# The opening of a decoder layer: one tile's modulation moved to TensorE, c spread by TensorE, small loads on ScalarE's queue, order of the splits fixed

## The chip, the cores and the metric

The kernel runs on one core of one Trainium2 chip. A core has TensorE (PE, matrix products; PEld is its loading of the stationary operand), VectorE (DVE), ScalarE (ACT), GpSimd (POOL) and SyncE (SP, which here only issues DMA transfers). The metric is the device time of one execution in microseconds, lower is better; the median of several runs is given. All numbers are in microseconds unless it is said otherwise.

## The reference, cut to what matters

The reference is one decoder layer on x (512 x 1024, float32) with a conditioning vector c (1024). What the change touches is at its very beginning:

```python
mod = c @ w_ada + b_ada                      # 1024 -> 6 * 1024
sh1, sc1, gt1, sh2, sc2, gt2 = split(mod, 6)
u = x * (1.0 + sc1) + sh1
proj = u @ w_in                              # q, k, v, forget logits, gates of two attention branches
log_f = log_sigmoid(f_a + b_forget)
# two causal attention branches (softmax with forget decay; stick-breaking),
# each projected to 1024, merged by sigmoid gates, times w_o
x = layer_norm(ALPHA * x + (1 + gt1) * attn_out)
u2 = x * (1.0 + sc2) + sh2
h = causal_depthwise_conv(u2 @ w_up)         # width 3
x = layer_norm(ALPHA * x + (1 + gt2) * ((silu(h_gate) * h_val) @ w_down))
```

So the first products with w_in need u, u needs sc1 and sh1, and these need c and two sixths of w_ada.

## The kernel before, in words

Products in float32 precision are made of three faster ones: each operand is split into a high part (a rounding copy, `hi_of`, on ScalarE) and a low part (the difference, `lo_of`, on VectorE), and high times high, high times low and low times high are added up in PSUM. Both helpers record one line for all their uses, so in the profile the splits are told apart by their tiles: `wh` and `wl` are the parts of a weight tile `raw`, `uh` and `ul` those of a tile of u.

The opening works on the eight channel tiles of 128 channels, j = 0 to 7. u is held with channels on partitions, so that scale and shift are one number per partition. For each j the kernel

- loads two 128 x 1024 tiles `wa` of w_ada (its transpose: one row per channel), the rows of x for these channels (`xt`, 128 x 512) and the first 904 columns of w_in (`raw`): `first_load`, all on SP's queue;
- sums each `wa` against c, which lies spread over all partitions in `cbc`, into one number per partition, and adds the bias: `first_acc` and `mod_col`, on VectorE. The result is `modc`;
- splits `raw`: `first_split`, and for the pieces that come late `first_pad`, which also fills the eight forget columns in `fpad`;
- makes `uh` on ScalarE from `xt` with scale and bias, then u in place of `xt` on VectorE, then `ul` as their difference: `first_mod`. The in-place u has to wait until ScalarE has read `xt`;
- issues 23 products, spread over eight PSUM banks (`grp`) that add up over j: `first_mm`.

For j = 0 the sums are made in two halves of 512 columns, as the pieces come in. The first half of `cbc` is loaded by a DMA that repeats the row of c over all partitions. The second half is spread by TensorE, a product of a row of ones and the row `cbr`, and copied out of PSUM by ScalarE.

The order on SP's queue is that of the program text. The order of the other engines is planned by a scheduler that works with its own costs; `tc.issue_after(x)` ties what is issued within it behind x. DMA transfers share a ring of eight semaphores, so that the ninth waits for the first. Tiles come from pools with a fixed number of buffers: five for `wa`, four for `raw` (`LOADS`), three for each of `wh` and `wl` (`WBUFS`).

Behind the opening come the attention heads, with further projections as filler between them, the merge and w_o, the first norm, the up projection with the convolution, and the down projection with the last norm. Their code isn't touched, but for `mod_col`, which later tiles of w_ada use as well and which loses a parameter that they don't set.

Of the kernel before, what the change touches and what calls it, by code (L numbers as in the profile page):

```python
# [8 lines left out]
F32 = mybir.dt.float32  # L9
F32R = mybir.dt.float32r  # L10
BF16 = mybir.dt.bfloat16
# [5 lines left out]
P = 128  # L17
# [21 lines left out]
LATE = 6  # L39
EARLY = 2  # L40
CUT = 5
FILL = (13, 13, 13), (11, 11, 11)


@with_exitstack
def layer_kernel(ctx: ExitStack, tc: tile.TileContext, out, xT, x, cT, crow, wa0, wa1, bcol, bgt, w1, wct, wv, bf,
                 wp, wo, lncol, lnrow, wup, cwb, wdn):
# [32 lines left out]
    cbc = const([P, D], F32, "cbc")  # L80
    cbr = early.tile([1, 512], F32, name="cbr", tag="cbr")
    nc.sync.dma_start(cbr, crow[:, 512:1024])
# [7 lines left out]
    S.activation(sgt, ones[:, 0:1], AF.Sigmoid)  # L90
    make_identity(nc, ident)
# [64 lines left out]
    G.memset(fl(fpad), 0.0)  # L156
    PE.matmul(grp[0], ones[0:1, :], cbr, start=True, stop=True)
    S.activation(cbc[:, 512:1024], grp[0], AF.Copy)

    def mod_col(w, col, wt, parts=1):  # L160
        raw = modr[:, w, col, :]
        n = D // parts
        for e in range(parts):
            c = slice(e * n, (e + 1) * n)
            V.scalar_tensor_tensor(wt[:, c], wt[:, c], 1.0, cbc[:, c], ALU.mult, ALU.mult, accum_out=raw[:, e : e + 1])
        b, o = bcols[:, w, col : col + 1], modc[:, w, col : col + 1]
        if parts == 1:
            V.tensor_tensor(o, raw[:, 0:1], b, ALU.add)
        else:
            V.scalar_tensor_tensor(o, raw[:, 0:1], raw[:, 1:2], b, ALU.add, ALU.add)  # L170

    def first_load(j):
        wa = [early.tile([P, D], F32, name=nm("wa"), tag="wa", bufs=5) for _ in range(2)]
        r = stg.tile([P, 1024], F32, name=nm("raw"), tag="raw", bufs=LOADS)
        xt = z(F32, "xt")
        if j == 0:
            for e in range(2):
                c = slice(e * 512, (e + 1) * 512)
                if e == 0:
                    nc.sync.dma_start(cbc[:, c], crow[:, c].broadcast_to([P, 512]))  # L180
# [4 lines left out]
            for c in (slice(0, 384), slice(384, W1C)):  # L185
                nc.sync.dma_start(r[:, c], w1[j][:, c])
            nc.sync.dma_start(cTs, cT)
            nc.sync.dma_start(bfs, bf)
        else:
            nc.sync.dma_start(r[:, 0:W1C], w1[j])  # L190
            nc.sync.dma_start(xt, xT[j * P : (j + 1) * P, :])
            for q in range(2):
                nc.sync.dma_start(wa[q], wa0[j, q])
        pend[j] = [wa, xt, r]

    def first_acc(j):
        wa = pend[j][0]
        if j == 0:
            for q in (1, 3):
                V.tensor_scalar_add(bcols[:, q, :], bcols[:, q, :], 1.0)  # L200
        mod_col(0, j, wa[0], 2 if j == 0 else 1)
        mod_col(1, j, wa[1], 2 if j == 0 else 1)

    def first_split(j):
        r = pend[j][2]
# [3 lines left out]
        if j:  # L209
            lo_of(l[:, 0:W1C], r[:, 0:W1C], h[:, 0:W1C])  # L210
        pend[j][2:] = [h, l, r]
# [11 lines left out]
    def first_mod(j):  # L223
        wa, xt = pend[j][0:2]
        sh, sc = modc[:, 0, j : j + 1], modc[:, 1, j : j + 1]
        a, b = z(F32R, "uh"), z(F32R, "ul")
        u = S.activation(a, xt, AF.Identity, bias=sh, scale=sc)
        V.tensor_scalar(xt, xt, sc, sh, ALU.mult, ALU.add)
        state["after"] = lo_of(b, xt, a)
        if j == 0:  # L230
            with tc.issue_after(u.ins):
                first_pad(j)
        else:
            first_pad(j)
        uh.append(a)
        ul.append(b)
# [746 lines left out]
def _pack(inputs):  # L983
# [18 lines left out]
    def col(kind, n):  # L1002
        if kind in ("sb", "fox"):
# [23 lines left out]

_NAMES = ["xT", "x", "cT", "crow", "wa0", "wa1", "bcol", "bgt", "w1", "wct", "wv", "bf", "wp", "wo", "lncol", "lnrow",
          "wup", "cwb", "wdn"]
# [19 lines left out]
```

## Time and profile before

| | |
|---|---|
| median of 3 runs | 772.62 us (772.52 to 773.3) |
| the profiled execution: time, and span of its core | 772.12 us, 770.3 us |
| TensorE busy | 748.1 us, 97% of the span |
| VectorE busy | 549.4 us, 71% |
| ScalarE busy | 350.4 us, 45% |
| GpSimd busy | 185.7 us, 24% |
| loaded from HBM | 96.88 MB |
| first product of channel tile 0 starts at | 10.46 us |
| first product of channel tile 7 starts at | 49.26 us |

The page of the profile gives each engine's busy time, then the span in 40 slices with the busy share in tenths. The timeline rows give the start, the length, the engine, the line of the code and the operation as out<-in, with the number of instructions that the row merges; in brackets stands the idle time of the engine before it and what ended that. The ends of products are modelled and overlap the next one's start, so the pace of products is read from their starts.

### The profile page before, as it was taken

The page shows a single profiled execution, that of the slowest core. Times are in us where ns is not written, and L with a number is a line of the kernel's source. Part 1 is how long each engine was busy: PE and PEld are TensorE (multiplying, and loading weights), DVE is VectorE, ACT ScalarE, POOL GpSimd, SP SyncE. Part 2 cuts the span into 40 slices and gives each one's busy share as a digit, 9 for nine tenths or more (in the row PEclk, how much of TensorE's full clock was granted, in tenths as well). Part 3 has the DMA queues.
Part 4 walks back from the last instruction along what each step waited for, and adds up shares of the span by engine and source line. Part 5 has one row for each costly group of instructions (what it writes and reads, how often), then busy time and mean ns, then how long its engine had stood idle before and what let it go on. Part 6 is the DMA issues. An engine that isn't in the chain of part 4 may idle for free.

```text
span 770.3 us, 9560 instructions
## 1 busy us (share of the span) xinstructions
PE 748.1 (97%) x3556; PEld 620.6 (81%) x3556; DVE 549.4 (71%) x822; ACT 350.4 (45%) x583; POOL 185.7 (24%) x138
## 2 busy tenths in 40 slices
PE   5998999999999999999999999999999999999995
PEld 3886887788888888888889888888888888888885
DVE  6979889966687977776676787686656665533666
ACT  3357686717667556333145434444444433222400
POOL 1025424510000011364000780000000043945500
PEclk9999999999999999999999999999999999999998
DMA  8951253542333323455302524354332214323202
GB/s 310 403 204 55 83 165 131 175 161 83 110 110 110 127 93 136 144 190 164 137 1 73 201 79 145 118 177 137 114 105 93 100 55 165 120 98 127 65 28 83
DMA packets 31105, 99.68 MB, mean 129 GB/s; under 512 B 4273, under 2 KB 4785, under 8 KB 31058
## 3 DMA queue, kind: packets, MB, share of 16 engines
q1 hardware_dynamic: 30546, 99.00, 37.0%
q8 instruction: 28, 0.46, 0.2%
q14 instruction: 19, 0.16, 0.1%
q0 software_dynamic: 512, 0.07, 0.1%
HBM read 96.88 MB, written 2.10 MB: 128 GB/s over the span
## 4 chain that ended last, share of the span: by engine, by line
PE 86%; DVE 6%; ACT 5%; DMA 1%; issue 1%; SPq 0%; DVEq 0%; ACTq 0%
PE ps L110 17%; PE ps L111 17%; PE ps L112 17%; PE ps L941 5%; PE ps L940 5%; PE ps L942 5%; PE ps L254 4%; PE ps L495 2%; PE ps L821 2%; PE ps L820 2%; PE ps L819 2%; PE ps L477 2%; DVE om L456 1%; DMA wa<-in_wa 1%; ACT wh L75 1%
## 5 line engine op out<-in xcount | busy, mean ns | idle before, releaser
L78 DVE TENSOR_TENSOR wl<-raw,wh 128x1024 fp32r<-128x1024 f32 (+2 forms) x106 | 143.8, 1357 | 101.0 <-ACT wh L75 100.5
L75 ACT ACTIVATE wh<-raw 128x1024 fp32r<-128x1024 f32 (+2 forms) x106 | 110.4, 1042 | 108.1 <-PE ps L942 39.9
L110 PE MATMUL ps<-u2h,wh 128*128 128x512 f32 (+1 forms) x376 | 141.4, 376 | 0.0
L111 PE MATMUL ps<-u2l,wh 128*128 128x512 f32 (+1 forms) x376 | 141.2, 376 | 0.0
L112 PE MATMUL ps<-u2h,wl 128*128 128x512 f32 (+1 forms) x376 | 141.2, 375 | 0.0
L587 POOL TENSOR_TENSOR raw<-raw,gt 128x1024 f32<-128x1024 f32 x22 | 60.7, 2774 | 187.1 <-DVE gt L550 157.6
L110 PE MATMUL ps<-uh,wh 128*128 128x512 f32 x232 | 92.9, 400 | 2.2 <-DVE vv L78 2.2
L112 PE MATMUL ps<-uh,wl 128*128 128x512 f32 x232 | 90.8, 391 | 0.0
L111 PE MATMUL ps<-ul,wh 128*128 128x512 f32 x232 | 90.8, 391 | 0.0
L110 PEld LDWEIGHTS ps<-u2h,wh 128*128 128x128 f32 x376 | 70.8, 188 | 12.9
L111 PEld LDWEIGHTS ps<-u2l,wh 128*128 128x128 f32 x376 | 70.8, 188 | 12.8
L112 PEld LDWEIGHTS ps<-u2h,wl 128*128 128x128 f32 x376 | 70.8, 188 | 12.6
L110 PEld LDWEIGHTS ps<-uh,wh 128*128 128x128 f32 x232 | 43.6, 188 | 10.7 <-DVE vv L78 2.5
L112 PEld LDWEIGHTS ps<-uh,wl 128*128 128x128 f32 x232 | 43.6, 188 | 9.4
L111 PEld LDWEIGHTS ps<-ul,wh 128*128 128x128 f32 x232 | 43.7, 188 | 7.9
L940 PE MATMUL ps<-wh,hh 128*128 128x512 f32 x128 | 49.8, 389 | 0.0
L941 PE MATMUL ps<-wl,hh 128*128 128x512 f32 x128 | 49.8, 389 | 0.0
L942 PE MATMUL ps<-wh,hl 128*128 128x512 f32 x128 | 49.8, 389 | 0.0
L457 POOL TENSOR_TENSOR pt<-pt,om 128x127 f32<-128x127 f32 (+3 forms) x32 | 40.0, 1278 | 33.8 <-DVE om L456 28.7
L75 ACT ACTIVATE hh<-cv 128x512 fp32r<-128x512 f32 x22 | 13.9, 631 | 59.6 <-DVE cv L920 59.6
L575 POOL TENSOR_TENSOR raw<-raw,gt 128x1024 f32<-128x1024 f32 x8 | 21.1, 2645 | 78.0 <-DVE m L78 42.2
L919 ACT ACTIVATE cv<-cv 128x512 f32<-128x512 f32 x22 | 13.9, 632 | 54.5 <-DVE cv L914 54.5
(188 smaller groups left out, 1463.0 us busy)
## 6 DMA issues: line engine op xcount, KB each, us to landing
raw<-in_wup SPq DMA_DIRECT2D x44, 512.0 KB, 3.3
raw<-in_wa SPq DMA_DIRECT2D x32, 512.0 KB, 3.3
raw<-in_wct SPq DMA_DIRECT2D x29, 512.0 KB, 3.2
raw<-in_wdn SPq DMA_DIRECT2D x22, 512.0 KB, 3.2
wa<-in_wa SPq DMA_DIRECT2D x14, 512.0 KB, 8.7
raw<-in_wp SPq DMA_DIRECT2D x8, 512.0 KB, 3.3
raw<-in_wo SPq DMA_DIRECT2D x8, 512.0 KB, 3.6
raw<-in_w SPq DMA_DIRECT2D x7, 452.0 KB, 8.3
```

What stands on the lines that cost most here:

```text
L75: S.activation(o, i, AF.Copy, scale=scale)
L78: return V.tensor_tensor(o, i, fl(hi), ALU.subtract)
L110: PE.matmul(ps, wh, ah, start=first, stop=False)
L111: PE.matmul(ps, wh, al, start=False, stop=False)
L112: PE.matmul(ps, wl, ah, start=False, stop=last)
L254: PE.matmul(grp[g], w, u, start=j == 0 and n == 0, stop=j == KT - 1 and n == (1 if g == 7 else 2))
L457: G.tensor_tensor(pt[b][:, s : e - 1], pt[b][:, s : e - 1], om[:, s + 1 : e], ALU.mult)
L575: G.tensor_tensor(r, r, gt[0], ALU.mult)
L587: G.tensor_tensor(r, r, gt[1], ALU.mult)
L940: PE.matmul(ps, hh[j][:, tb], w[0], start=first, stop=False)
L941: PE.matmul(ps, hh[j][:, tb], w[1], start=False, stop=False)
L942: PE.matmul(ps, hl[j][:, tb], w[0], start=False, stop=last)
```

## The change

Four things change, all in the opening:

1. The modulation of tile 0 is summed by TensorE. Its two tiles now come from w_ada itself (`wam`, contraction on partitions), and for each of shift and scale eight products of a 128 x 128 block with one column of c (`cTs`) add up in one column of a bank; VectorE adds the bias to both. They are in plain float32. `wa0` keeps the tiles 1 to 7.
2. c is spread by TensorE alone: a tile `crz` of zeros, with c in its first row, is multiplied by a 128 x 128 matrix of ones, in two products of 512 columns, and ScalarE copies both to `cbc`. VectorE zeroes `crz` (it takes one of the `wa` buffers), and the DMA of c waits for that. Before them stand three products on another zeroed tile (`WARM = 3`, bf16, 512 columns), whose result isn't used.
3. The small inputs (`cTs`, `bcols`, `bfs` and the row of c) are loaded on ScalarE's queue, ahead of its table load; SP's queue begins with the tiles of `wam`. For tile 1 the loads are put in another order.
4. The order on the engines is tied: the split of tile j + 1 behind `uh` of tile j on ScalarE, the sums of tile j + 1 behind `ul` of tile j on VectorE; for tile 1 its low parts behind its `modc`.

```diff
+    S.dma_start(cTs, cT)
...
+    S.dma_start(bcols, bcol)
+    crz = early.tile([P, D], F32, name="crz", tag="wa", bufs=5)
+    V.memset(crz, 0.0)
+    crd = S.dma_start(crz[0:1, :], crow)
+    warm = early.tile([P, 512], BF16, name="warm", tag="warm")
+    V.memset(warm, 0.0)
...
-    PE.matmul(grp[0], ones[0:1, :], cbr, start=True, stop=True)
-    S.activation(cbc[:, 512:1024], grp[0], AF.Copy)
...
+    for n in range(WARM):
+        PE.matmul(grp[4], warm[:, 0:P], warm, start=True, stop=True)
+    for e in range(2):
+        PE.matmul(grp[e], ones, crz[:, e * 512 : (e + 1) * 512], start=True, stop=True)
+        S.activation(cbc[:, e * 512 : (e + 1) * 512], grp[e], AF.Copy)
...
         if j == 0:
-            for e in range(2):
-                c = slice(e * 512, (e + 1) * 512)
-                if e == 0:
-                    nc.sync.dma_start(cbc[:, c], crow[:, c].broadcast_to([P, 512]))
-                for q in range(2):
-                    nc.sync.dma_start(wa[q][:, c], wa0[j, q][:, c])
-            nc.sync.dma_start(bcols, bcol)
+            for q in range(2):
+                for e in range(2):
+                    c = slice(e * 512, (e + 1) * 512)
+                    nc.sync.dma_start(wa[q][:, c], wam[q][:, c])
+            nc.sync.dma_start(r[:, 0:384], w1[j][:, 0:384])
             nc.sync.dma_start(xt, xT[j * P : (j + 1) * P, :])
...
+            nc.sync.dma_start(r[:, 384:W1C], w1[j][:, 384:W1C])
+            S.dma_start(bfs, bf)
+        elif j == 1:
+            nc.sync.dma_start(wa[0], wa0[j - 1, 0])
+            nc.sync.dma_start(r[:, 0:W1C], w1[j])
+            nc.sync.dma_start(wa[1], wa0[j - 1, 1])
+            nc.sync.dma_start(xt, xT[j * P : (j + 1) * P, :])
...
-        mod_col(0, j, wa[0], 2 if j == 0 else 1)
-        mod_col(1, j, wa[1], 2 if j == 0 else 1)
+            mps = grp[2]
+            for q in range(2):
+                for k in range(KT):
+                    PE.matmul(mps[:, q : q + 1], wa[q][:, k * P : (k + 1) * P], cTs[:, k : k + 1], start=k == 0, stop=k == KT - 1)
+            V.tensor_tensor(modc[:, 0:2, 0], mps[:, 0:2], bcols[:, 0:2, 0], ALU.add)
+            return
+        mod_col(0, j, wa[0])
+        state["modc"] = mod_col(1, j, wa[1])
...
+        if j == 1:
+            h, l, r = pend[j][2:]
+            with tc.issue_after(state["modc"].ins):
+                state["after"] = lo_of(l[:, 0:W1C], r[:, 0:W1C], h[:, 0:W1C])
         a, b = z(F32R, "uh"), z(F32R, "ul")
-        u = S.activation(a, xt, AF.Identity, bias=sh, scale=sc)
-        V.tensor_scalar(xt, xt, sc, sh, ALU.mult, ALU.add)
+        u = state["u"] = S.activation(a, xt, AF.Identity, bias=sh, scale=sc)
+        with tc.issue_after(state["after"].ins) if j == 1 else ExitStack():
+            V.tensor_scalar(xt, xt, sc, sh, ALU.mult, ALU.add)
         state["after"] = lo_of(b, xt, a)
-        if j == 0:
-            with tc.issue_after(u.ins):
-                first_pad(j)
-        else:
+        with tc.issue_after(u.ins):
             first_pad(j)
...
         if j + 1 < KT:
-            first_split(j + 1)
-            first_acc(j + 1)
+            with tc.issue_after(state["u"].ins) if j else ExitStack():
+                first_split(j + 1)
+            with tc.issue_after(state["after"].ins):
+                first_acc(j + 1)
...
-    r["wa0"] = c(wt[0:2].transpose(1, 0, 2, 3))
+    r["wa0"] = c(wt[0:2, 1:].transpose(1, 0, 2, 3))
+    r["wam"] = c(wk[:, :, 0:2, 0:P].transpose(2, 1, 0, 3).reshape(2, P, D))
```

More of the change, by code (lines that the diff above doesn't have):

```diff
@@ L40 @@
 EARLY = 2
+WARM = 3
 CUT = 5
@@ L45, in layer_kernel @@
 @with_exitstack
-def layer_kernel(ctx: ExitStack, tc: tile.TileContext, out, xT, x, cT, crow, wa0, wa1, bcol, bgt, w1, wct, wv, bf,
+def layer_kernel(ctx: ExitStack, tc: tile.TileContext, out, xT, x, cT, crow, wam, wa0, wa1, bcol, bgt, w1, wct, wv, bf,
                  wp, wo, lncol, lnrow, wup, cwb, wdn):
@@ L89, in layer_kernel @@
     sgt = const([P, 1], F32, "sgt")
-    S.activation(sgt, ones[:, 0:1], AF.Sigmoid)
+    with tc.issue_after(crd.ins):
+        S.activation(sgt, ones[:, 0:1], AF.Sigmoid)
     make_identity(nc, ident)
@@ L156, in layer_kernel, with mod_col @@
     G.memset(fl(fpad), 0.0)
-    PE.matmul(grp[0], ones[0:1, :], cbr, start=True, stop=True)
-    S.activation(cbc[:, 512:1024], grp[0], AF.Copy)
[L160 to L168, printed above, removed]
-        else:
-            V.scalar_tensor_tensor(o, raw[:, 0:1], raw[:, 1:2], b, ALU.add, ALU.add)
+    for n in range(WARM):
[3 more added lines that the diff above has]
+        S.activation(cbc[:, e * 512 : (e + 1) * 512], grp[e], AF.Copy)
+    def mod_col(w, col, wt):
+        raw = modr[:, w, col, 0:1]
+        V.scalar_tensor_tensor(wt, wt, 1.0, cbc, ALU.mult, ALU.mult, accum_out=raw)
+        return V.tensor_tensor(modc[:, w, col : col + 1], raw, bcols[:, w, col : col + 1], ALU.add)
     def first_load(j):
```

13 lines of the change are left out of this document (3 added, 10 removed).

## The prediction

> **What bounds the kernel now.** I read the page's engine shares first, then busy time by stretches of the opening, then the opening's timeline engine by engine, then the rows of the nearest priced instructions.
>
> ```profile
> span 770.3 us, 9560 instructions
> ...
> PE 748.1 (97%) x3556; PEld 620.6 (81%) x3556; DVE 549.4 (71%) x822; ACT 350.4 (45%) x583; POOL 185.7 (24%) x138
> ...
> PE   5998999999999999999999999999999999999995
> ```
>
> TensorE is the bound over the whole kernel; only the first slice (19 us) has a visible hole. A change of the opening is worth what it moves the moment from which TensorE runs without a hole. By stretches (columns: window, length, then busy us and instruction count of PE, PEld, DVE, ACT, POOL, granted clock, DMA share, GB/s):
>
> ```profile
> 10.50:17.40 6.90, 6.90 (x24) 5.31 (x24) 5.66 (x13) 2.47 (x6) 0.00 (x0) 1.00 1.01 374
> ...
> 28.20:33.40 5.20, 5.20 (x25) 4.30 (x24) 5.20 (x12) 1.88 (x3) 0.00 (x0) 1.00 1.03 402
> ```
>
> From 28 us on one channel tile (23 products) takes 5.20 us of a full TensorE. VectorE is full as well, and the DMA engines are. The first tile took 6.9. TensorE's own timeline, start and length in front:
>
> ```profile
> 2.24 2.04 PE L157 MATMUL ps<-cbr,ones 1*128 1x512 f32 x2 [2.24 <-DMA cbr<-in_crow]
> 10.46 1.65 PE L254 MATMUL ps<-uh,wh 128*128 128x512 f32 x3 [6.18 <-ACT uh L227]
> ...
> 13.89 0.62 PE L254 MATMUL ps<-wl,uh 128*128 128x512 f32 x2
> ```
> ```profile
> 49.26 0.39 PE L254 MATMUL ps<-uh,wh 128*128 128x512 f32 x1
> ```
>
> Tile 0 starts at 10.46. Its first eight products take 3.43 us, 0.43 each; after 13.89 the pace is 0.23 (5.20/23). The granted clock column says 1.00 for that window, so the slow start is read from the pace alone. The last tile (7) starts at 49.26, and everything behind it keeps its order in the changed kernel. So I forecast one number: when tile 7 starts after the change. What holds a tile's start is its `uh`, hence VectorE and ScalarE. From tile 1 to tile 2 they ran thus:
>
> ```profile
> 16.32 0.16 DVE L168 TENSOR_TENSOR modc<-modr,bcols 128x1 f32<-128x1 f32 x1
> 17.37 0.55 DVE L228 TENSOR_SCALAR xt<-xt,modc 128x512 f32<-128x512 f32 x1 [0.89 <-ACT uh L227]
> 17.95 0.69 DVE L78 TENSOR_TENSOR ul<-xt,uh 128x512 fp32r<-128x512 f32 x1
> 18.55 1.09 DVE L78 TENSOR_TENSOR wl<-raw,wh 128x904 fp32r<-128x904 f32 x1
> 19.56 1.22 DVE L165 SCALAR_TENSOR_TENSOR wa<-wa,cbc 128x1024 f32<-128x1024 f32 x1
> ...
> 22.00 0.15 DVE L168 TENSOR_TENSOR modc<-modr,bcols 128x1 f32<-128x1 f32 x1
> ```
> ```profile
> 16.52 0.82 ACT L227 ACTIVATE uh<-xt,modc 128x512 fp32r<-128x512 f32 x1 [4.30 <-DVE modc L168]
> ...
> 22.19 0.81 ACT L227 ACTIVATE uh<-xt,modc 128x512 fp32r<-128x512 f32 x1 [0.62 <-DVE modc L168]
> ```
>
> The sequence is modc, `uh` on ScalarE, then `xt` on VectorE (it overwrites what `uh` reads, hence the wait of 0.89), `ul`, the split of the next tile, two sums over wa, the next modc. It comes round in 22.19 - 16.52 = 5.67 us, more than TensorE's 5.20. Later in the old kernel VectorE goes another way: it puts `xt` and `ul` of the tile before between the sums, so nothing waits.
>
> ```profile
> 33.95 0.69 DVE L78 TENSOR_TENSOR ul<-xt,uh 128x512 fp32r<-128x512 f32 x1
> ...
> 38.58 0.69 DVE L78 TENSOR_TENSOR ul<-xt,uh 128x512 fp32r<-128x512 f32 x1
> ```
>
> That round takes 4.63 us, 0.57 less than TensorE, so VectorE runs ahead and TensorE is the bound.
>
> **The change, part by part.**
>
> *Order pinned.* The changed program's VectorE order is the same for every tile from 2 to 7: split, sum, sum, modc, pad, modc, `xt`, `ul`, next split; the next sums are tied behind this tile's `ul`. That is the 5.67 sequence, with the wait on `uh` in every round. Behind the waiting `xt` stand `ul`, the next split and the next sums, and the next `uh` waits for those. Tile 1 has its split under its `uh` and comes to the same. So `uh` of tile 7 starts 6 x 5.67 = 34.0 us after that of tile 1, and TensorE can no longer cover it: 5.67 against 5.20 is 0.47 lost per tile. From `uh` to the tile's first product are 0.87 (22.19 to the products at 23.06 in the trace; for tile 0 it ends likewise). Tile 7 starts at its old 49.26 only if `uh` of tile 1 starts at 49.26 - 0.87 - 34.0 = 14.4, where the old one starts at 16.52. The change in time is therefore (new start of `uh` of tile 1) - 14.4.
>
> *From modc of tile 0 (call it M) to that `uh`.* 0.20 (16.32 to 16.52), 0.85 (16.52 to 17.37), then `xt`, rest of split 0, `ul`, pad, which took 12.26 - 10.44 = 1.82, then two sums and modc, 22.19 - 19.56 = 2.63. Sum 5.5: the break-even M is 8.9.
>
> ```profile
> 7.10 0.69 DVE L165 SCALAR_TENSOR_TENSOR wa<-wa,cbc 128x512 f32<-128x512 f32 x1 [0.32 <-DMA wa<-in_wa]
> ...
> 10.44 0.55 DVE L228 TENSOR_SCALAR xt<-xt,modc 128x512 f32<-128x512 f32 x1
> ...
> 12.26 1.09 DVE L78 TENSOR_TENSOR wl<-raw,wh 128x904 fp32r<-128x904 f32 x1
> ...
> 13.71 1.23 DVE L165 SCALAR_TENSOR_TENSOR wa<-wa,cbc 128x1024 f32<-128x1024 f32 x1 [0.28 <-DMA wa<-in_wa]
> ```
>
> *What M waits for: loads.* The broadcast of c (256 KB by DMA) is gone, and SP's first big issue moves from 1.13 to 0.73. The four 256 KB pieces of w_ada land no later than the third did (fourth of the old stream, 7.10), less 0.4: 6.7. SP loses five issues, like the two rows below, of a queue that has to wait anyway. Its first raw piece now waits for a semaphore of the first four DMAs, while three pieces are still queued, so the stream doesn't run dry.
>
> ```profile
> 0.73 0.34 SPq L82 DMA_DIRECT2D cbr<-in_crow  x1
> 1.13 0.36 SPq L180 DMA_DIRECT2D cbc<-in_crow  x1
> ```
> ```profile
> cbc<-in_crow SPq DMA_DIRECT2D x1, 256.0 KB, 3.6
> ```
>
> *What M waits for: c.* VectorE zeroes 128x1024: no such row, but 128x512 takes 0.55 above, so 1.1, from 0.73 to 1.8. ScalarE's queue issues four DMAs; at SP's spacing of 0.4 the fourth, c's row, leaves at 1.9 and is behind the zeroing too. Behind it on ScalarE stand a table load and the first split, which wait for later loads anyway. Landing is bounded by 1.5 us (cbr, 0.73 to 2.24) and 3.6 (cbc): 3.4 to 5.5. I take 4.1, nearer the short one, since it is one row, but now beside a full stream.
>
> *The broadcast.* Two products of 512 columns in plain float32; the old one cost 2.04 at the slow pace, two passes of 1.02. The three products on the zeroed bf16 tile fill about 2.1 to 3.4 (0.43 each). In the old trace the pace rose after 3.4 us of work (10.46 to 13.89); from 2.1 that is 5.5, so I count two passes at 1.02 and two at 0.51: 4.1 + 3.1 = 7.2. Bounds: 2.0 and 4.1. The copies of cbc on ScalarE, at most as long as a `uh` (0.82) each, end by 8.9 and are covered by what follows.
>
> *The sum by TensorE.* 16 products with one column each, in plain float32, so 32 passes, each with a load of 128 columns. The trace has no one-column product; the nearest are the float32 transposes and the slow L157:
>
> ```profile
> L477 PEld LDWEIGHTS ps<-ident,pt x10: 140/141/143, 75.2 to 76.3; 128*128 128x128 f32 x10
> L477 PE MATMUL ps<-ident,pt x10: 272/272/273, 75.4 to 76.4; 128*128 128x128 f32 x10
> ```
> ```profile
> L157 PEld LDWEIGHTS ps<-cbr,ones x2: 282/305/328, 2.2 to 2.4; 1*128 1x128 f32 x2
> ```
>
> Ten transposes start within 1.0 us, 0.11 apart, with a weight load each. 32 x 0.11 = 3.5 us, so the sum ends at 10.7 and M is 10.9 with 0.2 for the handover. Bounds: half of that if the load alone counts (a load of 141 ns partly overlapped), and twice that, 7.0, at the slow pace, since the slow loads are 282 to 328 ns against 141. The Trainium skill, "TensorE: Matmul & The Clock Gate", section "LDWEIGHTS (loading the stationary operand)", gives a load as its columns over 1.2, 107 ns, with no word of the clock; by that the sum would take 3.4 us in either state and the slow case below would fall away. The two rows, 282 and 141, speak against it.
>
> VectorE loses four half sums (0.69 each) and gains 1.4 of zeroing and a modc, all before M, where it waits. A faster start of tile 0 by a warm TensorE is worth nothing at the end: at 6.9 instead of 5.2 us the tile would end 1.7 late, and the 0.47 per tile that TensorE gains on `uh` absorbs that by tile 5.
>
> **The sum.** M 10.9, `uh` of tile 1 at 16.4, less 14.4: +2.0 us. The profiled execution took 772.12 (span 770.3), 0.5 under the median of 772.62; I put the +2.0 on the median: 774.6.
>
> **Rivals.** *The slow clock lasts.* The pause from 3.4 to 4.1 lets the count begin anew, or products of one column don't count as work. For it: the old broadcast (2.0 us of work) left tile 0 slow. All four broadcast passes then take 4.1 (to 8.2), and the sum 3.5 to 7.0: M 11.9 to 15.4, change +3.0 to +6.5, typically +4.5: 777.1. The Trainium skill, same page, section on the HAM clock gate, says that activity is judged in windows of about 3.4 us which run freely; as an estimate from that page the rise could come as late as 8.9, inside this range; the old trace's 3.4 agrees with it as far as one start can.
>
> *The sum is quick and loads bind.* If one-column passes run at half of 0.11, M is at 8.9 or below. Up to the second wa of tile 1 both programs move the same 3.2 MB, counted from the shapes (old: up to the first wa, landed 13.71), and the stream starts 0.4 earlier: 13.3; a sum and modc on top (1.23 + 0.2) give `uh` at 14.8, +0.4: 773.0. Against it: no row prices a load under 0.1.
>
> *The pinned order costs nothing.* If `xt` doesn't wait, or VectorE's round is below 5.20 (the wait would have to shrink from 0.89 to 0.42), TensorE's pace rules: tile 0 starts at M + 1.1 = 12.0, tile 7 7 x 5.2 later at 48.4, -0.9: 771.7, and with a quick sum (M 8.9) -2.9: 769.7. For it: the old kernel's second half of the opening. Against it: the wait of `xt` on ScalarE stands in the changed program for each tile.
>
> **How the numbers follow.** Chances: forecast 0.55 (own range +0.9 to +3.0), slow clock 0.20, quick sum 0.12, no cost of the order 0.12, something else 0.01. The range leaves out the no-cost rival below (0.12) and the upper third of the slow clock above (0.07): 773.0 to 778.3 (+0.4 to +5.7). A measurement tells 0.2%, 1.55 us, from no change. Slower than that: three quarters of the forecast's case and the slow clock, 0.61. Within: the rest of the forecast's, the quick sum, half of the no-cost case, 0.33. Faster: 0.06.
>
> **What would show it.** Right: `xt` waits on `uh` by about 0.9 in every tile; starts of `uh` 5.6 to 5.7 apart; TensorE idle about 0.4 before each tile; modc of tile 0 near 10.9; tile 7 starting near 51.3. Wrong, if tile starts are 5.2 apart, if modc of tile 0 comes before 9 or after 13, or if the time goes after tile 7.

## The result and the profile after

The changed kernel is slower: 779.54 us, median of 4 runs (776.78 to 780.83), against 772.71 for the kernel before beside it (4 runs, 772.52 to 773.3). The ratio is 1.0082 with a 95% interval from 1.0055 to 1.011. The profiled execution took 779.55, 7.43 more than that of before (772.12). The runs of the changed kernel are spread over 4 us, those of before over 0.8.

The engine shares and slices of the page of after, which answer to the first lines shown of before:

```profile
span 777.7 us, 9630 instructions
...
PE 758.6 (98%) x3593; PEld 629.2 (81%) x3593; DVE 550.3 (71%) x815; ACT 349.9 (45%) x584; POOL 184.5 (24%) x138
...
PE   7998999999999999999999999999999999999995
```

TensorE is busier by 10.5 us in a span longer by 7.4, and the first slice looks fuller (7 instead of 5). A busy share tells nothing here of progress: the first slice is full of work that the kernel before did elsewhere, and that runs slowly. The time is lost before the attention stage begins. The first product behind the opening (line 110 before, 117 after) starts at 54.48 and at 61.74, 7.26 later, and from there to the end the two traces run in step (the distance stays between 7.2 and 7.3). The two rows, before and after:

```profile
54.48 0.47 PE L110 MATMUL ps<-uh,wh 128*128 128x512 f32 x1
```
```profile
61.74 0.44 PE L117 MATMUL ps<-uh,wh 128*128 128x512 f32 x1
```

TensorE's timeline of after, start and length in front (a product in plain float32 stands there as two instructions, which are called passes here):

```profile
2.26 1.46 PE L165 MATMUL ps<-warm 128*128 128x512 bf16 x3 [2.26 <-DVE warm L90]
5.35 3.75 PE L167 MATMUL ps<-crz,ones 128*128 128x512 f32 x4 [1.63 <-DMA crz<-in_crow]
8.89 6.83 PE L208 MATMUL ps<-cTs,wa 128*128 128x1 f32 x32
16.82 1.65 PE L266 MATMUL ps<-uh,wh 128*128 128x512 f32 x3 [1.10 <-ACT uh L241]
...
20.40 0.69 PE L266 MATMUL ps<-wl,uh 128*128 128x512 f32 x2
...
23.90 0.84 PE L266 MATMUL ps<-uh,wh 128*128 128x512 f32 x3
...
56.23 0.50 PE L266 MATMUL ps<-uh,wh 128*128 128x512 f32 x1 [0.17 <-ACT uh L241]
```

Read from top to bottom: c lands at 5.35, the spread of c ends at 8.89, the sum of 32 passes takes 6.8 more, `uh` of tile 0 follows, and tile 0 starts at 16.82 (10.46 before). Tile 7 starts at 56.23 (49.26 before, +6.97). The remaining 0.3 falls between there and 61.74: behind the wait for `uh` tile 7's own first products start further apart than before.

The pace of TensorE is slow from 2.26 to about 20.4: tile 0's first eight products take 3.58 (16.82 to 20.40), and only then does the pace double. The weight loads of the sum (durations as shortest/median/longest in ns), and three stretches (columns as in the table of windows of before):

```profile
L208 PEld LDWEIGHTS ps<-cTs,wa x32: 333/334/337, 8.0 to 15.3; 128*128 128x128 f32 x32
```
```profile
5.35:8.89 3.54, 3.54 (x4) 1.48 (x5) 0.10 (x1) 0.66 (x2) 0.00 (x0) 1.00 0.95 279
8.89:16.82 7.93, 6.83 (x34) 6.74 (x32) 0.77 (x4) 1.71 (x4) 0.00 (x0) 1.00 1.00 381
...
29.11:34.33 5.22, 5.22 (x25) 4.32 (x23) 4.30 (x10) 1.68 (x3) 0.00 (x0) 1.00 0.82 279
```

The column of the granted clock (the first of the last three) says 1.00 in all three, as it did before; in these two traces the slow pace can be read from starts and durations alone. The last row answers to the window 28.20 to 33.40 of before: TensorE is as full as it was, but VectorE is busy for 4.30 of 5.22 instead of 5.20, because it now waits. Its rows and those of ScalarE:

```profile
15.76 0.16 DVE L209 TENSOR_TENSOR modc<-ps,bcols 128x2 f32<-128x2 f32 x1 [6.41 <-PE ps L208]
...
27.82 0.55 DVE L243 TENSOR_SCALAR xt<-xt,modc 128x512 f32<-128x512 f32 x1 [0.89 <-ACT uh L241]
...
33.50 0.55 DVE L243 TENSOR_SCALAR xt<-xt,modc 128x512 f32<-128x512 f32 x1 [0.89 <-ACT uh L241]
```
```profile
21.25 0.82 ACT L241 ACTIVATE uh<-xt,modc 128x512 fp32r<-128x512 f32 x1 [3.01 <-DVE modc L173]
26.97 0.82 ACT L241 ACTIVATE uh<-xt,modc 128x512 fp32r<-128x512 f32 x1 [3.95 <-DVE modc L173]
...
55.37 0.81 ACT L241 ACTIVATE uh<-xt,modc 128x512 fp32r<-128x512 f32 x1 [2.97 <-DVE modc L173]
```

VectorE waits 6.41 for the sum, and then 0.89 for `uh` in each round from tile 2 on. `uh` starts 5.68 apart: (55.37 - 26.97) / 5.

### The profile page after: what moved, and what is told of

Its sections match the earlier page's. It is cut to its first block, busy times and chain, and to the rows that moved or that the text cites. A ratio compares the mean times of both kernels' runs of the same rounds, so it can differ in the third digit from the quotient of the medians.

```text
span 777.7 us, 9630 instructions
## 1 busy us (share of the span) xinstructions
PE 758.6 (98%) x3593; PEld 629.2 (81%) x3593; DVE 550.3 (71%) x815; ACT 349.9 (45%) x584; POOL 184.5 (24%) x138
## 4 chain that ended last, share of the span: by engine, by line
PE 83%; DVE 8%; ACT 5%; DMA 2%; issue 2%; ACTq 0%; SPq 0%; DVEq 0%
PE ps L117 17%; PE ps L118 17%; PE ps L119 17%; PE ps L955 5%; PE ps L954 5%; PE ps L956 5%; PE ps L509 2%; PE ps L834 2%; PE ps L835 2%; PE ps L833 2%; PE ps L491 2%; DVE wa L172 2%; DVE wl L79 2%; DVE om L470 1%; ACT wh L76 1%
## 5 line engine op out<-in xcount | busy, mean ns | idle before, releaser
L79 DVE TENSOR_TENSOR wl<-raw,wh 128x1024 fp32r<-128x1024 f32 (+2 forms) x106 | 149.0, 1406 | 101.8 <-ACT wh L76 101.2
L119 PEld LDWEIGHTS ps<-u2h,wl 128*128 128x128 f32 x376 | 70.9, 188 | 12.6
```

What stands on the lines that cost most here:

```text
L79: return V.tensor_tensor(o, i, fl(hi), ALU.subtract)
L119: PE.matmul(ps, wl, ah, start=False, stop=last)
```

## The experiments

The theory after the result: the pinned order and the late modc of tile 0 (M) act as the prediction says, and M is so late because the sum is done at TensorE's slow pace, behind a late c. The rivals: one-column passes cost 0.21 at any pace; the order costs nothing and TensorE's late start alone decides; a fast TensorE in tile 0 would pay after all.

Where a starting time is compared, "before" is the first trace (tile 0 at 10.46, `uh` of tile 1 at 16.52, tile 7 at 49.26). The kernel before was run beside each group on the same chip: its median was 772.95 for the first four experiments below, 773.79 for the fast TensorE, the sum alone, the float32 products and the version without the tie, and 773.2 for the mixed sum, the version with the tie and the control. Ratios are to these.

**Twelve products ahead instead of three.** The products on the zeroed bf16 tile, whose result isn't used, fill TensorE until after c has landed.

```diff
-WARM = 3
+WARM = 12
```

> The changed kernel with 12 instead of 3 products on the zeroed tile, so that TensorE works without a break from 2.3 us until c has landed (5.35) and beyond. Theory A (the sum by TensorE is dear because the clock is still slow; in the trace of the changed kernel its 32 passes stand 0.21 apart and the first products of tile 0, too, are slow): the pace rises at about 5.7, the broadcast starts at about 6.5 and takes 2.0 instead of 3.75, the 32 passes stand 0.11 apart and end near 12, modc of tile 0 comes near 12.2 instead of 15.76, tile 7 starts 3.5 earlier; time 775.5 to 776.5. Theory B (a one-column float32 pass costs 0.21 whatever the clock): the passes stay 0.21 apart, they start at 8.5 and modc stays at 15.3 or later; time 779 to 780. Theory C (one-column products let the clock fall again): the passes begin 0.11 apart and go over to 0.21; time between, 777 to 778.5.

Measured: 777.98 (777.62 to 779.8), ratio 1.0066, interval 1.0051 to 1.0081. TensorE's rows of this kernel:

```profile
7.35 2.17 PE L167 MATMUL ps<-crz,ones 128*128 128x512 f32 x4
9.37 3.63 PE L208 MATMUL ps<-cTs,wa 128*128 128x1 f32 x32
14.09 1.10 PE L266 MATMUL ps<-uh,wh 128*128 128x512 f32 x3 [1.10 <-ACT uh L241]
14.99 1.05 PE L266 MATMUL ps<-wh,uh 128*128 128x512 f32 x2
```
```profile
L208 PEld LDWEIGHTS ps<-cTs,wa x32: 190/192/192, 8.9 to 12.7; 128*128 128x128 f32 x32
```
```profile
15.00:17.00 2.00, 2.00 (x6) 1.61 (x5) 2.00 (x4) 0.51 (x1) 0.00 (x0) 0.50 1.03 411
```

The same 32 passes take 3.6 instead of 6.8, 0.11 each instead of 0.21, so the passes have no fixed price; the pace sets it. That is theory A's mechanism, and theory B falls. `uh` of tile 1 starts at 18.52, which by the prediction's rule (less 14.4) gives +4.1; tile 7 starts at 53.48, +4.2. Tile 0 begins fast at 14.09 and falls back to the slow pace within a microsecond (1.05 for two products). Here the granted clock shows it: the column reads 1.00 from 9.0 to 14.5 and 0.50 from 15 to 17. Theory C's fall thus came too, but behind the sum. The time misses theory A's range (775.5 to 776.5): the pace rose during the spread and not at 5.7, the spread began at 7.35 and not at 6.5, so tile 7 came 2.75 earlier than in the changed kernel and not 3.5, and the profiled execution loses another 1.1 at about 310 us, in untouched code (see the control).

**Tile 0's sum on VectorE, the rest as changed.** `wam` then holds the transposed tiles, and the two sums are made over 1024 columns.

```diff
-            mps = grp[2]
-            for q in range(2):
-                for k in range(KT):
-                    PE.matmul(mps[:, q : q + 1], wa[q][:, k * P : (k + 1) * P], cTs[:, k : k + 1], start=k == 0, stop=k == KT - 1)
-            V.tensor_tensor(modc[:, 0:2, 0], mps[:, 0:2], bcols[:, 0:2, 0], ALU.add)
-            return
...
-    r["wam"] = c(wk[:, :, 0:2, 0:P].transpose(2, 1, 0, 3).reshape(2, P, D))
+    r["wam"] = c(wt[0:2, 0])
```

> The changed kernel, but tile 0's modulation is summed by VectorE again (its two tiles in the old layout, whole tiles against cbc); warm-up, broadcast by TensorE, loads and pinned order stay. Theory A (the sum on TensorE is the largest part): cbc is complete near 9.8, two sums of 1.15 give modc near 12.3 instead of 15.76, uh of tile 1 near 17.8, tile 7 near 52.8; time 775.5 to 776.5. If the pinned order were the largest part instead: within 1 us of the changed kernel, 778.5 to 779.5.

Measured: 777.13 (776.66 to 777.65), ratio 1.0051, interval 1.0036 to 1.0066.

```profile
5.42 3.75 PE L167 MATMUL ps<-crz,ones 128*128 128x512 f32 x4 [1.70 <-DMA crz<-in_crow]
13.52 1.65 PE L260 MATMUL ps<-uh,wh 128*128 128x512 f32 x3 [4.35 <-ACT uh L235]
```
```profile
9.84 1.23 DVE L172 SCALAR_TENSOR_TENSOR wa<-wa,cbc 128x1024 f32<-128x1024 f32 x1 [1.73 <-ACT cbc L168]
```

Tile 0 starts at 13.52. Against 16.82 this prices the sum on TensorE at 3.30; against 10.46 it prices the new way of c at 3.06, with no sum on TensorE at all. Not all of the 3.06 is the way of c: the two whole-tile sums (1.15 apart) can start only when the second half of `cbc` is copied, at 9.84, where with sums in halves, as in the kernel before, two of 0.61 would be left by then. By that estimate about 1.1 belongs to the whole tiles and some 2 to the way of c. `uh` of tile 1 starts at 17.95 (+3.55 by the rule), tile 7 at 52.90 (+3.64; 52.8 was expected). The time was expected at 775.5 to 776.5 and came out 0.6 above; the profiled execution loses 0.6 at about 217 us, in untouched code.

**The pinned order alone, in the kernel before.**

```diff
-        u = S.activation(a, xt, AF.Identity, bias=sh, scale=sc)
+        u = state["u"] = S.activation(a, xt, AF.Identity, bias=sh, scale=sc)
...
-            first_split(j + 1)
-            first_acc(j + 1)
+            with tc.issue_after(state["u"].ins) if j else ExitStack():
+                first_split(j + 1)
+            with tc.issue_after(state["after"].ins):
+                first_acc(j + 1)
```

> The kernel before with the pinned order alone (split of the next tile behind uh of this one, its sums behind ul of this one), everything else as before. Theory A: uh of tile 1 stays at 16.5, from there the starts of uh stand 5.67 apart instead of TensorE's 5.2, tile 7 starts at 51.4 instead of 49.26; time 774.5 to 775.2, ratio near 1.0027. Rival: VectorE's slack hides the wait and the time stays at 772.7.

Measured: 774.69 (774.51 to 776.13, 10 runs), ratio 1.0027, interval 1.0017 to 1.0037. ScalarE's and TensorE's rows:

```profile
16.68 0.81 ACT L227 ACTIVATE uh<-xt,modc 128x512 fp32r<-128x512 f32 x1 [4.33 <-DVE modc L168]
22.36 0.82 ACT L227 ACTIVATE uh<-xt,modc 128x512 fp32r<-128x512 f32 x1 [1.46 <-DVE modc L168]
...
50.73 0.81 ACT L227 ACTIVATE uh<-xt,modc 128x512 fp32r<-128x512 f32 x1 [3.06 <-DVE modc L168]
```
```profile
51.59 0.50 PE L254 MATMUL ps<-uh,wh 128*128 128x512 f32 x1 [0.16 <-ACT uh L227]
```

`uh` of tile 1 is where it was (16.68), the rounds are 5.67 apart, (50.73 - 22.36) / 5, and tile 7 starts at 51.59, 2.33 late; the rule gives 16.68 - 14.4 = 2.28. The order has a price of its own, and the rival that it costs nothing falls.

**The changed kernel without the ties for tiles 2 to 7.**

```diff
-            with tc.issue_after(state["u"].ins) if j else ExitStack():
-                first_split(j + 1)
-            with tc.issue_after(state["after"].ins):
+            first_split(j + 1)
+            with ExitStack() if j else tc.issue_after(state["after"].ins):
                 first_acc(j + 1)
```

> The changed kernel without the ties for tiles 2 to 7 (those of tile 1 stay). Theory A: modc of tile 0 stays near 15.8, tile 0 runs at the slow clock until 23.9, and from there TensorE sets the pace (5.2 per tile), so tile 7 starts at 55.2 instead of 56.23; only 1.0 to 1.3 us are won back: 778.2 to 778.5. Rival (the order is what costs, not the late modc): 3 us or more won back, 776.5 or less.

Measured: 777.61 (776.01 to 779.32), ratio 1.0057, interval 1.0036 to 1.0078.

```profile
16.57 1.65 PE L266 MATMUL ps<-uh,wh 128*128 128x512 f32 x3 [1.10 <-ACT uh L241]
24.16 0.84 PE L266 MATMUL ps<-uh,wh 128*128 128x512 f32 x3
...
55.44 0.39 PE L266 MATMUL ps<-uh,wh 128*128 128x512 f32 x1
```

Without the ties TensorE is the bound from tile 0 on, at 5.21 a tile, and tile 7 still starts at 55.44, 6.2 late: a start at 16.57 and a slow tile 0 (7.59, until 24.16) are enough for that. Of the 6.97 of the changed kernel the ties therefore add only 0.8 in the end, by these two traces. The times alone would not decide it: they spread from 776.0 to 779.3, around the theory's 778.2 to 778.5 and down to the rival's 776.5 or less. The two losses overlap; their prices (2.3 for the order, the rest for M) don't add up but hide each other.

**A fast TensorE in tile 0, in the kernel before.** Twelve products on a zeroed tile, whose result isn't used, stand behind the spread of c.

```diff
+    warm = early.tile([P, 512], BF16, name="warm", tag="warm")
+    V.memset(warm, 0.0)
...
+    for n in range(12):
+        PE.matmul(grp[4], warm[:, 0:P], warm, start=True, stop=True)
```

> The kernel before with twelve products on a zeroed bf16 tile behind the spread of c, in the idle stretch of TensorE from 4.3 to 10.5; their result isn't used. It isolates the fast clock of tile 0 with no change of order. The prediction's claim (a faster start of tile 0 is worth nothing at the end): tile 0's 23 products take about 5.3 us instead of 6.9, TensorE then waits about 1.6 us for uh of tile 1, which still starts near 16.5, tile 7 starts within 0.2 of 49.26 and the time is 772.5 to 773.2 (ratio 0.9995 to 1.0005). Rival (TensorE's time is the bound from tile 0 on): tile 7 starts 1.6 earlier and the time is 771.0 to 771.6. Second rival (the clock falls again, or the products delay tile 0): slower by up to 1 us.

Measured: 774.62 (773.65 to 776.16, 11 runs), ratio 1.0018, interval 1.0008 to 1.0027.

```profile
4.13 4.73 PE L162 MATMUL ps<-warm 128*128 128x512 bf16 x12
10.32 0.96 PE L258 MATMUL ps<-uh,wh 128*128 128x512 f32 x3 [1.46 <-ACT uh L231]
...
17.55 0.98 PE L258 MATMUL ps<-uh,wh 128*128 128x512 f32 x3 [1.73 <-ACT uh L231]
```

Tile 0 runs at the fast pace, TensorE then waits 1.73, tile 1 starts at 17.55, and tile 7 at 49.43 (+0.17). In the opening the gain is nothing, as the prediction claimed. The time is still 0.2% (0.8) longer, as the second rival had it, but not by its mechanism: the pace didn't fall and tile 0 wasn't late. In the profiled execution the loss comes in steps in the attention stage, at about 144, 217, 307 and 369 us, where this kernel has no edit; see the control below. The wait of 1.46 ahead of tile 0 didn't bring the slow pace back.

**The sum on TensorE alone, in the kernel before.** c is spread as before; the pieces of w_ada are loaded tile by tile, and `cTs` on ScalarE's queue.

```diff
+    S.dma_start(cTs, cT)
...
-        mod_col(0, j, wa[0], 2 if j == 0 else 1)
-        mod_col(1, j, wa[1], 2 if j == 0 else 1)
+            mps = grp[2]
+            for q in range(2):
+                for k in range(KT):
+                    PE.matmul(mps[:, q : q + 1], wa[q][:, k * P : (k + 1) * P], cTs[:, k : k + 1], start=k == 0, stop=k == KT - 1)
+            V.tensor_tensor(modc[:, 0:2, 0], mps[:, 0:2], bcols[:, 0:2, 0], ALU.add)
+            return
+        mod_col(0, j, wa[0])
+        mod_col(1, j, wa[1])
...
+    r["wam"] = c(wk[:, :, 0:2, 0:P].transpose(2, 1, 0, 3).reshape(2, P, D))
```

> The kernel before with one part of the change alone: tile 0's modulation is summed by TensorE (16 products of one column, 32 passes), c is spread as before and the order isn't tied. Theory (the passes are priced by the slow clock): 32 passes of 0.21 from about 5.5, or from the landing of the last piece near 7; the first modc of tile 0 between 12.2 and 12.8 instead of 8.9, uh of tile 1 near 18, tile 7 between 50.5 and 51.5, time 774.0 to 775.2. Rival (0.11 a pass as the prediction has it, since the clock depends on what ran before): modc near 9.7, tile 7 within 0.5 of 49.26, time 772.3 to 773.3.

Measured: 777.3 (776.79 to 778.26), ratio 1.0049, interval 1.0036 to 1.0061.

```profile
5.87 6.96 PE L203 MATMUL ps<-cTs,wa 128*128 128x1 f32 x32 [1.65 <-DMA wa<-in_wam]
13.94 1.65 PE L259 MATMUL ps<-uh,wh 128*128 128x512 f32 x3 [1.10 <-ACT uh L232]
```

The passes are slow again (7.0 for 32), modc of tile 0 starts at 12.87, `uh` of tile 1 starts at 19.62, and tile 7 at 52.45, 3.2 late. That is more than the theory named (50.5 to 51.5, and 774.0 to 775.2 for the time), because I took `uh` of tile 1 at 18: without the changed order of tile 1 the way from modc of tile 0 to that `uh` is 6.75 (12.87 to 19.62), against 5.49 in the changed kernel (15.76 to 21.25). That part of the change does save 1.3.

**What raises the pace: plain float32 products ahead.** The three products ahead are in plain float32, on a zeroed tile; their result isn't used.

```diff
-    warm = early.tile([P, 512], BF16, name="warm", tag="warm")
+    warm = early.tile([P, 512], F32, name="warm", tag="warm")
```

> The changed kernel with its three products on a zeroed tile of 512 columns in plain float32 in place of bf16, so twelve full-width passes of about 0.88 from 2.3 on, and then the spread of c; their result isn't used. It tells why 10 us of work didn't raise the pace. If full-width float32 passes raise it as others do and only the one-column ones don't count: the passes go from about 0.88 to 0.45 between 5.5 and 7.2, the twelve end near 9 to 10, the spread takes about 2 and the sum 3.6; the time is near 779 to 780. If plain float32 work doesn't raise it at all: twelve passes take 10.6, the spread 3.6 and the sum 6.8 behind that, modc of tile 0 near 23.5 and the time near 787.

Measured: 777.41, one run. I had miscounted: a float32 product is two passes (as in the old spread), so these are six passes and not twelve.

```profile
2.52 4.45 PE L165 MATMUL ps<-warm 128*128 128x512 f32 x6 [2.52 <-DVE warm L90]
6.81 1.88 PE L167 MATMUL ps<-crz,ones 128*128 128x512 f32 x4
8.53 3.63 PE L208 MATMUL ps<-cTs,wa 128*128 128x1 f32 x32
13.25 1.65 PE L266 MATMUL ps<-uh,wh 128*128 128x512 f32 x3 [1.10 <-ACT uh L241]
```
```profile
12.00:13.25 1.25, 0.15 (x2) 0.07 (x1) 0.31 (x3) 0.86 (x2) 0.00 (x0) 0.75 1.03 408
13.25:19.40 6.15, 6.15 (x15) 4.79 (x16) 6.12 (x14) 3.14 (x6) 0.00 (x0) 0.50 1.04 410
```

Six slow passes at 0.85 would take over 5 us; they took 4.3, so the pace rose among them, and the spread and the sum are fast. Plain float32 with 512 columns counts as work. Here too tile 0 is slow again (1.65 for three products), and the granted clock reads 0.50 for its first 6.15 us. In the window ahead of it the column reads 0.75, half of 1.00 and half of 0.50, so the fall came at about 12.6: 4.1 after the last full-width product (the sum follows it at 8.53), of which 3.6 are one-column passes and only 0.5 a pause.

**Full-width products between the one-column ones.** The kernel with twelve products ahead, and one more behind each product of the sum.

```diff
                     PE.matmul(mps[:, q : q + 1], wa[q][:, k * P : (k + 1) * P], cTs[:, k : k + 1], start=k == 0, stop=k == KT - 1)
+                    PE.matmul(grp[4], warm[:, 0:P], warm, start=True, stop=True)
```

> The kernel with twelve products ahead, and in tile 0's sum one product of 512 columns on the zeroed bf16 tile behind each of the 16 products of one column; their result isn't used. With twelve products alone the pace fell 0.8 into tile 0, some 5.5 after the last full-width product. If one-column products don't count as work and full-width ones do: the pace stays fast, the sum takes 16 x 0.44 = 7.0 from 9.4, so it ends near 16.5, uh of tile 0 starts near 16.8, and tile 0's first 20 products take 4.5 to 4.6 at 0.23 throughout. If the fall has another cause (time since the start, the copies, the pause ahead of tile 0): it falls near 14.9 all the same, or in tile 0's first microsecond, and tile 0 takes over 6.5.

Measured: 779.57, one run.

```profile
14.70 0.38 PE L209 MATMUL ps<-warm 128*128 128x512 bf16 x1
15.94 0.96 PE L267 MATMUL ps<-uh,wh 128*128 128x512 f32 x3 [0.86 <-ACT uh L242]
16.73 0.62 PE L267 MATMUL ps<-wh,uh 128*128 128x512 f32 x2
```

The pace holds: tile 0's products start 0.23 apart from the second on, though more time has passed than with twelve products alone. The sum took 5.7 (9.26 to 14.9) and not 7.0, since a one-column product and a full-width one together take 0.36. So one-column products, 3.6 us of them without a hole, don't hold the fast pace, and in the changed kernel 6.8 us of them don't bring it about. The pause behind the sum isn't what ends the pace: it was 0.9 here, 1.46 with the fast TensorE in the kernel before, and the pace held in both.

**A version meant to beat both, in two steps.** c's row comes first on SP's queue, both halves of `cbc` are spread by TensorE from that one row, ten products on a zeroed tile (result not used) follow, VectorE makes tile 0's sums in halves, tile 1 has the changed order, tiles 2 to 7 aren't tied. The second version adds one tie, the last lines of the diff. The core of both against the kernel before:

```diff
+    cbr = early.tile([1, D], F32, name="cbr", tag="cbr")
+    nc.sync.dma_start(cbr, crow)
...
+    for e in range(2):
+        PE.matmul(grp[e], ones[0:1, :], cbr[:, e * 512 : (e + 1) * 512], start=True, stop=True)
+        S.activation(cbc[:, e * 512 : (e + 1) * 512], grp[e], AF.Copy)
+    for n in range(WARM):
+        PE.matmul(grp[4], warm[:, 0:P], warm, start=True, stop=True)
...
+            with tc.issue_after(state["u"].ins) if j == 1 else ExitStack():
+                first_split(j + 1)
```

> A version put together from what the runs before showed: c's row is the first transfer on SP's queue, both halves are spread by TensorE from one row, ten products on a zeroed bf16 tile keep TensorE at work until tile 0, tile 0's modulation is summed by VectorE in halves as in the kernel before, tile 1 keeps the changed kernel's order (its sums ahead of its low parts), tiles 2 to 7 aren't tied. If only uh of tile 1 and TensorE's pace behind it count: the pieces of w_ada land about 0.8 earlier, modc of tile 0 near 8.0 (8.9 before), uh of tile 1 near 14.2 (16.5 before), tile 7 between 46.8 and 48.0 (49.26 before), time 770.3 to 771.9. Rival (the loads of tiles 1 and 2 bind, since the DMA engines were full): uh of tile 1 between 15 and 16.5, tile 7 within 1 us of 49.26, time 772 to 773.5.

> The version with early sums and one tie more: the split of tile 2 stands behind uh of tile 1 on ScalarE. Without it the split waited for its load in front of uh of tile 1, whose modc was ready at 14.2 and which started at 15.6. If the order on ScalarE was what held it: uh of tile 1 starts near 14.4 (16.5 in the kernel before), tile 1's products near 15.3, tile 7 between 46.9 and 47.6 (49.26 before, 48.33 without the tie), and the time is 1 us under that of the version without the tie, some 1.5 to 2.3 under the kernel before (ratio 0.997 to 0.998). Rival: the loads of tile 2 bind behind it, so that tile 7 starts at 48 or later and the time is within 0.1% of the kernel before.

Measured, without the tie: 773.31 (772.43 to 774.16, 11 runs), ratio 0.9996, interval 0.9987 to 1.0005, no difference. `uh` of tile 1 starts at 15.63, tile 7 at 48.33, 0.9 early; that is between theory and rival, and the rest of the trace takes it back by 2.2 in the steps named above. ScalarE's rows around `uh` of tile 1:

```profile
14.76 0.96 ACT L76 ACTIVATE wh<-raw 128x904 fp32r<-128x904 f32 x1 [2.15 <-DMA raw<-in_w]
15.63 0.80 ACT L244 ACTIVATE uh<-xt,modc 128x512 fp32r<-128x512 f32 x1
```

A split that waits for its load stands ahead of a `uh` whose modc was ready at 14.2. With the tie: 774.98 (773.41 to 776.14, 7 runs), ratio 1.0027, interval 1.0016 to 1.0039, slower. The tie does what it should (`uh` of tile 1 at 14.16), and what follows is worse: the next sum waits for its load (0.85, VectorE at 16.44), VectorE's order for tile 2 changes with it, the next `uh` comes at 21.69 and tile 7 at 49.14. The rival came true for tile 7 (48 or later); its time (within 0.1% of the kernel before) did not, nor did the gain of 1 us over the version without the tie. None of the kernels beats the one before.

**The control.** The kernel before, unedited, profiled again.

> The kernel before, without an edit, profiled once more. In the last runs the offset against its first trace was constant from the opening to 130 us in every kernel, and then grew by 1.1 to 2.6 us in steps at 144, 217, 307 and 369 us (the attention stage), in kernels whose code there is untouched, while two kernels of the first runs (the changed one, and the order alone) show no such step. If the steps belong to the single execution or the chip and not to the edits: this trace shows steps at the same places, or its time lies at one end of a spread of 1 to 2 us of the kernel before. If they belong to the edits: its time is 772.1 to 772.9 and no step exceeds 0.2.

Measured: 772.9 (772.6 to 773.79, 8 runs), ratio 1.0, interval 0.999 to 1.001. Its profiled execution took 773.36, 1.24 over the first trace. Of that 0.8 arises in the opening (`uh` of tile 1 at 17.30 instead of 16.52), 0.2 to 0.3 at about 370 us and 0.15 near the end. One step, then, appears in untouched code of the same program, but a smaller one than in the experiments (the fast TensorE in tile 0 lost 2.65 behind the opening). Whether those larger steps come from the chip, from the single execution or from the shifted start, these runs don't settle. The column of the granted clock reads 1.00 around 144, 217, 307 and 369 us in the kernels that lose time there, so the steps are no slower clock that it shows. The opening itself also differs between executions of the same code: tile 0 took 6.9 in the first trace, 7.5 here and 7.6 with the order alone, as the pace rose earlier or later in it. Differences below about 1 us between single traces are not read here as effects of an edit, and the gains of 0.9 above, which the times don't show, stay open.

## Why the prediction was wrong

The direction, the price of the tied order and the rule from `uh` of tile 1 to the time were right; M itself was not, because TensorE's pace was taken wrongly. The forecast of 774.6 was 5 us too low; 779.54 also lies above the upper end of the range, 778.3. By the prediction's own steps:

- **Order pinned: right.** 5.68 a round, the wait of 0.89 in each, shown by the trace of after and by the order alone (+2.3 at tile 7, +1.7 in the time). One reading behind it was not exact: in the later rounds of the kernel before it is mainly the split of the next tile, standing ahead of `xt` (22.07 to 23.08), that fills the wait for `uh`; only `ul` stands between the two sums of a tile.
- **The rule, new start of `uh` of tile 1 less 14.4: right.** It gives 21.25 - 14.4 = +6.85 for the changed kernel, where tile 7 came 6.97 later and the time was 6.8 (medians) to 7.4 (profiled) longer; for four of the five experiments with the tied order it is within 0.1 as well (2.28 and 2.33, 3.55 and 3.64, 4.12 and 4.22, 5.94 and 6.03). With the float32 products it gives 3.28 where tile 7 came 3.53 later: there tile 0 took 8.26, and TensorE's own chain ended last. I expected TensorE to idle 0.4 ahead of each tile. It does so only ahead of the last tiles (the trace shows 0.17, and the first products behind it start further apart), because slow tile 0 ends late and the rounds catch up with it at tile 5 to 6. That is the absorption which the prediction named for tile 0, and the fast tile 0 in the kernel before (tile 7 +0.17) bears it out.
- **From modc of tile 0 to that `uh`, 5.5: right,** 15.76 to 21.25 is 5.49.
- **What M waits for, loads: not decisive.** The 32 passes run from 8.89 without a hole, so no piece was late.
- **What M waits for, c: mis-sized.** Landed at 5.35, not 4.1. The row was issued at 2.27, not 1.9, and took 3.1 to land (the short row of before took 1.5); I had taken a value near the lower bound, and the measured one is near the upper (5.5).
- **The broadcast: mis-sized.** All four passes were slow, 3.54 instead of 3.1, so it ended at 8.9 and not 7.2.
- **The sum by TensorE: the step that failed.** 6.8 instead of 3.5, close to the slow bound of 7.0 that I had named and not taken. "In the old trace the pace rose after 3.4 us of work" was read as a clock that starts with any work and then stays. The full-width work here was 1.5 us from 2.26 on, a pause of 1.6, and 3.5 more, and that didn't raise the pace; the one-column passes behind it don't count, as the mixed sum shows. So the pace stayed slow until 3.6 us into tile 0.

The sum of the three: 1.25 for c, 0.45 for the broadcast and 3.3 for the sum are 5.0, and M was 15.76 instead of 10.9, 4.9 later. The rival "The slow clock lasts" came true at its far end and a little beyond (M up to 15.4, +6.5, 779.1); it had 0.20 and the range cut its upper third off. Of its two conditions the second holds: one-column products don't count as work. The first, that the pause lets the count begin anew, wasn't tested by itself. Had I put the doubt on the sum, where both rows of the weight load stood at hand (282 to 328 slow, 141 fast), the slow case would have been the likelier: the one rise in the trace of before that I had read came in work without holes. One sum of the prediction is off by itself: by its own terms a quick sum gives M 9.15 (7.2, 1.75 and 0.2), not 8.9 or below; nothing above rests on it.

The estimate that I drew from the Trainium skill, "TensorE: Matmul & The Clock Gate", section on the HAM clock gate, let the rise come by 8.9 at the latest; the trace has it at 20.4, because the one-column products kept TensorE occupied without counting (the mixed sum). The Trainium skill, "TensorE: Matmul & The Clock Gate", section "LDWEIGHTS (loading the stationary operand)", gives a load of 128 columns as 107 ns with no word of the clock; the runs show 333 to 337 at the slow pace (the changed kernel) and 190 to 192 at the fast one (twelve products ahead) for the same 32 loads, with the passes 0.21 and 0.11 apart.

Where the 7 us come from, by the kernels above, read at tile 0's first product: the new way of c, with tile 0's sums over whole tiles, moves it by 3.06 (10.46 to 13.52; some 2 of them the way of c, by the estimate above), the sum on TensorE by 3.30 more (to 16.82). From there two chains run side by side. TensorE's own, 7.1 for a slow tile 0 and 5.2 for each further one, would by itself put tile 7 5.9 late (6.2 in the changed kernel without the ties, where tile 0 took 7.59). The chain of `uh`, 5.5 to `uh` of tile 1 (1.3 less than without the changed order of tile 1) and 5.68 a round, puts it 6.97 late; it ends last and decides.

## What to carry to other kernels

Work moved to an idle engine is priced at the pace that the engine has at that moment: ahead of TensorE's first dense stage that was the slow one in these kernels, unless enough full-width products stood ahead, and 32 tiny passes then cost 6.8 us on the path, where VectorE had made the sums as the loads came in. Price a small operand by its whole way (zeroing, issue, landing, spread, copy): here that way cost some 2 us by the estimate above, against 3.3 for the sum. And a tie that makes one engine wait for another in each round costs the difference of the round times, unless something else is late already; undoing it shows its price only in a kernel where nothing else is.

## What the hardware showed that I had not expected

- Plain float32 products with one moving column and a weight load each cost 0.11 us a pass at TensorE's fast pace and 0.21 at its slow one. In the latter they went on for 6.8 us without raising the pace; after 3.6 us of them at the fast pace it fell (4.1 us after the last full-width product in one kernel, 5.4 in another), and with a full-width product behind each two passes it held.
- The pace rose 3.2 to 6.2 us after work with 512 columns and all 128 rows had begun, where no one-row passes stood directly ahead: about 3.2, 4.6 and 4.9 in tile 0 of three executions of the same opening (the first trace of before, the control, the order alone), 3.6 in the changed kernel, 3.3 with the float32 products, 5.1 to 5.8 with twelve products ahead (from 2.26; the first pass of the spread, at 7.35, still took 0.73), and 6.2 in tile 0 behind the float32 products. Full-width work of 3.5 us was not enough in the changed kernel. In the two versions meant to beat both, ten products follow a spread from one row; there it rose 2.7 and 5.2 after the first of the ten, 6.4 and 8.9 after the first pass of the spread. Whether one-row passes count isn't tested.
- The profile's column of the granted clock reads 1.00 up to the first rise, though the pace is half: up to there the slow pace is seen in the starts of products and the durations of weight loads alone. A later fall does show, as 0.50, in the two kernels whose pace fell again in the opening (twelve products ahead, float32 products ahead).
